# Sixty counting instructions on VectorE and on ScalarE ahead of the first batch of a matmul kernel

## Chip, cores and metric

One core of one Trainium2 chip. The metric is the device time of one execution in microseconds (us). The span is the time from the first to the last instruction in the trace; for this kernel it is some 2 us shorter than the time (260.2 beside 262.41 us in the profiled run of before).

## The reference

```python
x: (16, 768, 512) float32;  y: (16, 768, 1024) float32
np.einsum('bkm,bkn->bmn', x, y).astype(np.float32)      # (16, 512, 1024)
```

Sixteen independent matmuls. Per batch 1.57 MB of x and 3.15 MB of y are read and 2.10 MB written.

## The kernel before

SyncE issues all transfers. VectorE casts x and y to bf16, GpSimd passes the casts' signals on to PE, PE multiplies in two groups of 24 matmuls a batch (48 in all), ScalarE copies each group from PSUM to a buffer that SyncE stores. There are two input buffers, two bf16 buffers, two PSUM halves and five output buffers.

```python
# SyncE
for b in range(B):
    i = b % 2
    if b >= 2:
        nc.sync.wait_ge(cast, nx[b - 2])                 # x buffer has been cast
    wide_dma("x", xs[i][:], x_v[b], 4, True).then_inc(sx[i], 16)
    if b >= 2:
        nc.sync.wait_ge(cast, nx[b - 2] + parts(b - 2))  # y buffer has been cast
    wide_dma("y", ys[i][:], y_v[b], 2, True).then_inc(sy[i], 16)
    if b >= LAG:                                         # LAG = 4
        store(b - LAG)
# ... the last four stores follow
# VectorE
for b in range(B):
    # ... waits for the bf16 buffer (b >= 2) and for x
    nc.vector.tensor_copy(xb[:, i], xs[i][:]).then_inc(cast, 1)
    nc.vector.wait_ge(sy[i], n)
    # ... cast of y, in two parts in the last batch
# ... GpSimd, PE
# ScalarE
nc.scalar.nop().then_inc(room, 2)
for b in range(B):
    # ... waits for the output buffer (b >= NO)
    for g in range(2):
        nc.scalar.wait_ge(groups, 2 * b + g + 1)
        cp = nc.scalar.copy(ob[b % NO][...], ps[g][:])   # cut
        # ... signals
```

## Time and profile before

| | before |
|---|---|
| time, median of the first 3 runs | 262.47 us (262.26 to 262.50) |
| span of the profiled run | 260.2 us |
| bytes moved, mean rate | 109.05 MB, 419 GB/s |
| busy: PE, VectorE, ScalarE | 73%, 32%, 23% |
| first matmul, last copy starts, last store issued | 18.51, 249.35, 251.24 us |

### The profile page before, as it was taken

How to read it: one execution, taken by the hardware profiler on the slowest of the kernel's cores; microseconds unless marked ns; L12 is line 12 of the kernel's file. 1: busy time of each engine (PE TensorE's matmuls, PEld its weight loads, DVE VectorE, ACT ScalarE, POOL GpSimd, SP SyncE). 2: the span in 40 equal slices, each digit the busy share in tenths (PEclk: the TensorE clock that was granted, in tenths of full speed). 3: DMA queues.
4: the chain of work that ended last, by engine and by line, in shares of the span. 5: the costliest groups of instructions: out<-in, count | busy, mean ns of one | idle time of the engine just before them, and what ended most of it. 6: DMA issues, size and time to landing. Idle time of an engine off the chain costs nothing. (4 is left out here: it accounts for less than half of the span.)

```text
span 260.2 us, 2386 instructions
## 1 busy us (share of the span) xinstructions
PE 189.0 (73%) x768; PEld 90.4 (35%) x768; DVE 82.0 (32%) x33; ACT 61.0 (23%) x33; POOL 0.2 (0%) x4
## 2 busy tenths in 40 slices
PE   0019999997938949689494995939869196796930
PEld 0004555553513514334241352514434043352510
DVE  0271644525241152411425214252232523125000
ACT  1000432343220220403222022220412214022220
POOL 0000000000000000000000000000000000000000
PEclk9999999999995977979889597997999889797995
DMA  7998989999999999998999989999998999999995
GB/s 272 434 487 378 484 378 468 393 358 479 423 395 471 385 474 431 426 433 385 489 416 426 448 368 461 418 463 408 393 496 378 466 446 411 433 393 436 423 408 232
DMA packets 4512, 109.05 MB, mean 419 GB/s; under 512 B 768, under 2 KB 768, under 8 KB 768
## 3 DMA queue, kind: packets, MB, share of 16 engines
q1 hardware_dynamic: 4512, 109.05, 98.3%
HBM read 75.50 MB, written 33.55 MB: 419 GB/s over the span
## 5 line engine op out<-in xcount | busy, mean ns | idle before, releaser
L146 PE MATMUL ps<-yb,xb 128*128 x768 | 189.0, 412 | 60.3 <-PEq L141 58.3
L146 PEld LDWEIGHTS ps<-yb,xb 128*128 x768 | 90.4, 118 | 158.5 <-issue 93.2
L160 ACT COPY ob<-ps 128x2048 f32<-128x2048 f32 x32 | 59.8, 1868 | 189.2 <-PE ps L146 189.2
L124 DVE CAST yb<-ys 128x6144 bf16<-128x6144 f32 (+1 forms) x17 | 53.8, 3171 | 86.8 <-DMA ys<-in_y_dram 86.8
L120 DVE CAST xb<-xs 128x3072 bf16<-128x3072 f32 x16 | 28.1, 1759 | 69.4 <-DMA xs<-in_x_dram 65.2
L160 ACT ACT_TABLE_LOAD x1 | 1.3, 1283 | 1.0 <-SPq L45 1.0
L184 POOL MEMSET const-bfloat16-1.0<- 128x1 bf16 x1 | 0.1, 101 | 0.0
L184 POOL MEMSET const-uint8-127<- 128x1 uint8 x1 | 0.1, 101 | 0.0
L184 POOL MEMSET const-float32-0.0<- 128x1 f32 x1 | 0.1, 98 | 0.2 <-issue 0.2
L184 POOL MEMSET const-float32-1.0<- 128x1 f32 x1 | 0.1, 98 | 0.0
## 6 DMA issues: line engine op xcount, KB each, us to landing
ys<-in_y_dram SPq DMA_DIRECT2D x16, 3072.0 KB, 28.2
out_dram<-ob SPq DMA_DIRECT2D x16, 2048.0 KB, 32.6
xs<-in_x_dram SPq DMA_DIRECT2D x16, 1536.0 KB, 29.8
```

The lines of the kernel that those rows point to most:

```text
L120: nc.vector.tensor_copy(xb[:, i], xs[i][:]).then_inc(cast, 1)
L124: nc.vector.tensor_copy(yb[:, i, ks], ys[i][:, ks]).then_inc(cast, 1)
L146: mm = nc.tensor.matmul(ps[g][:, m, nt], x_w[:, bass.ds(s, 1), kt, mo], yb[:, bass.ds(s, 1), kt, nt * NF:(nt + 1) * NF], start=(kt == 0), ...
L160: cp = nc.scalar.copy(ob[b % NO][:, g * HB:(g + 1) * HB].rearrange("p m (t f) -> p m t f", f=NF), ps[g][:])
L184: nc = _bacc.Bacc("TRN2", target_bir_lowering=False, num_devices=1)
```

## The change

VectorE and ScalarE have nothing to do until the first loads land. The change lets each run through 60 instructions that only add 1 to a semaphore for which nobody waits. The intent is to occupy both engines' sequencers in idle time; by design no wait, transfer or arithmetic is altered. Only ScalarE's table load, which stands behind the count, comes later (5.34 instead of 0.97 us).

```diff
+    idle = ec(nc.semaphore("idle"))
...
+    for _ in range(60):
+        nc.vector.sem_inc(idle, 1)
     for b in range(B):          # VectorE's loop
...
     nc.scalar.nop().then_inc(room, 2)
+    for _ in range(60):
+        nc.scalar.sem_inc(idle, 1)
     for b in range(B):          # ScalarE's loop
```

## The prediction

> **What bounds the kernel now.** I read the page from the top: busy shares first, then the DMA queue, then the start and the end of the run in order of time, because the change touches only the start.

> ```profile
> PE 189.0 (73%) x768; PEld 90.4 (35%) x768; DVE 82.0 (32%) x33; ACT 61.0 (23%) x33; POOL 0.2 (0%) x4
> ...
> DVE  0271644525241152411425214252232523125000
> ACT  1000432343220220403222022220412214022220
> ...
> DMA  7998989999999999998999989999998999999995
> ...
> q1 hardware_dynamic: 4512, 109.05, 98.3%
> HBM read 75.50 MB, written 33.55 MB: 419 GB/s over the span
> ```

> The two engines that get the new instructions are the idle ones: VectorE (DVE) is busy 32% of the span, ScalarE (ACT) 23%, and in the first slice of 6.5 us neither has any arithmetic (ACT's 1 is its table load). The DMA row is at 8 or 9 tenths everywhere but in the first and the last slice, and the queue takes 98.3% of sixteen engines' time. The bytes bound this kernel: 109.05 MB at the measured 419 GB/s is the 260.2 us span. VectorE and ScalarE matter only where they would make the queue run dry, at its head, or make the last store late, at its tail.

> The timeline of the first 32 us, cut to the loads and the two engines (columns: start us, duration us, engine, line, what it does, and in brackets its idle time and what ended it):

> ```profile
> 0.95 0.39 SPq L71 DMA_DIRECT2D xs<-in_x_dram  x1
> 0.97 1.28 ACT L160 ACT_TABLE_LOAD   x1 [0.97 <-SPq L45]
> ...
> 2.43 0.70 SPq L71 DMA_DIRECT2D ys<-in_y_dram  x1
> 7.26 1.76 DVE L120 CAST xb<-xs 128x3072 bf16<-128x3072 f32 x1 [7.26 <-DMA xs<-in_x_dram]
> 9.05 0.47 SPq L71 DMA_DIRECT2D xs<-in_x_dram  x1
> 14.57 3.36 DVE L124 CAST yb<-ys 128x6144 bf16<-128x6144 f32 x1 [5.55 <-DMA ys<-in_y_dram]
> ...
> 25.79 1.87 ACT L160 COPY ob<-ps 128x2048 f32<-128x2048 f32 x1 [23.54 <-PE ps L146]
> ```

> All four first loads are issued by SyncE with no wait, by 2.43 + 0.70 = 3.13 us. VectorE's first cast waits for data until 7.26 us, its second until 14.57 us. ScalarE loads its table and then has nothing until 25.79 us. Those are the two windows into which the change puts its instructions. The end is set by the last batch: the chain of work that ended last names only PE and ScalarE's copies, from 222.58 us on, and neither engine's stretch there is touched.

> [...]every transfer is in q1, issued by SyncE alone, so no VectorE or ScalarE instruction issues a transfer, before or after. [...]In this trace's DMA records the instruction fetches (six packets of 8192 bytes) all end more than 7 us before the first instruction; none lies in the span.[...]

> **The change, part by part.** Nothing is removed and no wait is added: nobody waits on the new semaphore. Built, the program has exactly 60 more semaphore instructions on VectorE (17 to 77) and on ScalarE (15 to 75); the order of casts, copies, matmuls and DMAs is unchanged on every engine.

> What one costs. The only semaphore records of the two engines inside the loop are their plain waits:

> ```profile
> L119 DVEq EVENT_SEMAPHORE  x14: 21/21/21, 29.3 to 227.5; - x14
> L159 ACTq EVENT_SEMAPHORE  x11: 17/17/17, 86.9 to 244.2; - x11
> ```

> They last 21 and 17 ns. From the start of such a wait to the start of the cast or copy behind it is 63 to 65 ns on VectorE and 56 to 61 ns on ScalarE where the data was there; two semaphore instructions in a row on GpSimd stand 78 ns apart. A VectorE record is 21/17 = 1.24 times as long, so the slow estimate for VectorE is 78 x 1.24 = 97 ns.
> - VectorE: 60 x 64 = 3.8 us to 60 x 97 = 5.8 us. Its last start-up branch is at 0.77 us and ends by 0.82, so the count ends at 4.7 to 6.6 us. The first cast can start at 7.26: hidden, with 0.6 to 2.6 us to spare.
> - ScalarE: 60 x 57 = 3.4 us to 60 x 78 = 4.7 us, from 0.9 us on. The table load (1.28 us) stands behind the count in the built order, so it ends at 5.6 to 6.9 us, against a first copy at 25.79. The increment by which ScalarE frees both PSUM halves stands ahead of the count, and PE does not start before 18.51 us anyway. Hidden by some 19 us.
> - On the path: 0. The sum is 0 us.

> Even if VectorE's count overran, the first cast has slack. It may start 5.55 us late and still be done when the second cast's data comes at 14.57 us. What it releases is the third x load, issued at 9.05 us behind three loads that are still queued: the cast of the second y starts at 25.57 us on data that only then lands. So per instruction the change would cost nothing until about (7.26 + 5.55 - 0.82) / 60 = 200 ns each, twice my slow estimate.

> **The rivals.**
> - *The count overruns the first load, and the end moves with it.* For it: the first cast is the earliest thing that VectorE does, and my slow estimate leaves only 0.6 us. Against: the slack of 5.55 us just shown. It would take over 200 ns each; at 250 ns, 60 x 250 = 15 us, the first y cast would start at about 15.8 + 1.8 = 17.6 us, 3 us late, and the time would be 265 us at the most, since the queue stays fed.
> - *Instruction fetch.* VectorE's program grows from 59 to 119 instructions, ScalarE's from 57 to 117; with what the runtime puts ahead that may need one more 8192-byte packet, or two. For it: [...]if it fell in the middle of the run, one cast or copy could be late by the time of a few queued packets (1.8 us for one of 49152 bytes). Against: [...]the queue holds two further loads (28.2 us from issue to landing). 0 to 2 us, most likely 0.
> - *It helps.* [...]For it I find nothing: the first cast starts when its load is complete, and no idle time before it is put down to issue.[...]
> - [...]

> **Range and chances.** The three runs before lie within 0.24 us, so what is left is noise and the small fetch risk, upward only. I predict 262.5 us, 261.9 to 263.2. A gain of 2% would be 5.2 us, [...]by an edit that feeds no transfer sooner: chance 0.01. A loss of 2% needs a stall of over 5 us that reaches the tail: 0.02. Same: 0.97.

> **What would show it right or wrong.** Right: 60 semaphore records on each engine, VectorE's ending before 7.26 us; the first cast still within 0.1 us of 7.26 and still waiting for the load; the table load at about 4.3 to 5.6 us; DMA share 98 to 99%, first matmul at about 18.5 us, last copy at about 249.3 us. Wrong: a first cast put down to issue, an instruction fetch inside the span with a gap on VectorE or ScalarE beside it, or a tail moved by over a microsecond.

The forecast's sum on the path was 0 us, and it stands. Passages of the prediction that no trace of this case shows are cut, and the cuts marked; none of them was a term of that sum.

## More of the kernel before

The lines for the start are in the prediction. For the end, which the prediction read too quickly, here are two stretches of the kernel before. The columns are the stretch, its length, the busy time of PE, its weight loads, VectorE, ScalarE and GpSimd (with counts), the granted clock of PE as a share of full speed, the DMA share and GB/s:

```profile
236.00:242.00 6.00, 4.93 (x15) 2.12 (x16) 2.17 (x2) 0.99 (x1) 0.00 (x0) 0.72 1.02 434
...
248.00:254.00 6.00, 1.31 (x7) 0.45 (x4) 0.00 (x0) 1.86 (x1) 0.00 (x0) 1.00 0.96 410
```

The second line is the one to keep: while PE does its last seven matmuls and ScalarE its last copy, the DMA engines are 96% busy, up to 252 us with stores of earlier batches. The first says that in this run PE was granted 0.72 of its clock early in the last batch.

## The result and the profile after

262.13 us median of 6 runs (261.94 to 262.59), beside 262.32 us of before (6 runs, 262.12 to 262.50). The ratio is 0.9995, 95% interval 0.9982 to 1.0007: the same. (Ratios here are the mean time of one kernel's fast runs over that of the other's of the same rounds, so not quite the ratio of the medians quoted.)

The page of the changed kernel, its DMA row and its queues:

```profile
DMA  7999989999999999999999999999999999999995
...
q1 hardware_dynamic: 4512, 109.05, 98.3%
q14 instruction: 2, 0.02, 0.0%
```

The share of the data queue is 98.3% as before. The last line is new: two packets that fetch instructions, inside the span. The trace has them at 9.01 and 10.84 us, 8192 bytes each.

The counting instructions, as groups by line (L116 is VectorE's loop, L159 ScalarE's; durations in ns, minimum, median and maximum, then first and last start in us):

```profile
L116 DVEq EVENT_SEMAPHORE  x60: 21/21/21, 1.0 to 6.4; - x60
L159 ACTq EVENT_SEMAPHORE  x60: 17/17/17, 1.0 to 5.3; - x60
```

From start to start they stand 92.8 ns apart on VectorE and 67.5 on ScalarE, though a record is only 21 and 17 ns long. In one place ScalarE paused: 376 ns between its 59th and 60th count.

The timeline of the start (start, duration, engine, what, idle time before and what ended it):

```profile
5.34 1.28 ACT L165 ACT_TABLE_LOAD   x1 [5.34 <-issue]
7.23 1.76 DVE L123 CAST xb<-xs 128x3072 bf16<-128x3072 f32 x1 [7.23 <-DMA xs<-in_x_dram]
9.01 0.47 SPq L72 DMA_DIRECT2D xs<-in_x_dram  x1
14.91 3.36 DVE L127 CAST yb<-ys 128x6144 bf16<-128x6144 f32 x1 [5.92 <-DMA ys<-in_y_dram]
...
18.85 13.36 PE L149 MATMUL ps<-yb,xb 128*128 x52 [18.85 <-PEq L144]
```

The first cast still waits for its load and starts at 7.23 us (7.26 before). The second starts at 14.91 instead of 14.57, and the first matmul at 18.85 instead of 18.51: the second load landed a third of a microsecond later. In the casts that shift is gone from the fifth batch's second cast on; the last copy starts at 249.33 us (249.35 before).

So three things were to be tested: how much counting the start really hides and by what; whether the fetches cost anything, and where; and what the same instructions cost on the chain that ends last.

### The profile page after: what moved, and what is told of

The parts are those of the page before. It is cut to its first block, busy times and chain, and to the rows that moved or that the text cites. A ratio compares the mean times of both kernels' runs of the same rounds, so it can differ in the third digit from the quotient of the medians.

```text
span 260.2 us, 2506 instructions
## 1 busy us (share of the span) xinstructions
PE 188.3 (72%) x768; PEld 90.3 (35%) x768; DVE 82.0 (32%) x33; ACT 61.1 (23%) x33; POOL 0.2 (0%) x4
## 3 DMA queue, kind: packets, MB, share of 16 engines
q1 hardware_dynamic: 4512, 109.05, 98.3%
HBM read 75.50 MB, written 33.55 MB: 419 GB/s over the span
## 5 line engine op out<-in xcount | busy, mean ns | idle before, releaser
L123 DVE CAST xb<-xs 128x3072 bf16<-128x3072 f32 x16 | 28.2, 1760 | 69.7 <-DMA xs<-in_x_dram 65.2
## 6 DMA issues: line engine op xcount, KB each, us to landing
ys<-in_y_dram SPq DMA_DIRECT2D x16, 3072.0 KB, 28.2
```

## The experiments

Twelve kernels ran. All gave the reference's result.

| run | edit | median us | before, same rounds | ratio (95% interval) |
|---|---|---|---|---|
| c0 | semaphore only, no counts | 262.40 | 262.49 | 1.0002 (0.9989 to 1.0015) |
| v60 | 60 on VectorE | 262.34 | 262.30 | 1.0010 (0.9981 to 1.0039) |
| a60 | 60 on ScalarE | 262.51 | 262.30 | 1.0017 (0.9984 to 1.0049) |
| mid30 | 30 on each | 261.90 | 262.30 | 0.9994 (0.9972 to 1.0017) |
| tail14 | 14 and 15 | 261.79 | 262.29 | 0.9977 (0.9963 to 0.9990) |
| tail14b | the same again | 262.30 | 262.49 | 0.9991 (0.9978 to 1.0004) |
| c120 | 120 on each | 262.44 | 262.29 | 1.0000 (0.9987 to 1.0014) |
| c240 | 240 on each | 265.55 | 262.29 | 1.0121 (1.0105 to 1.0137) |
| c480v | 480 on VectorE | 288.54 | 262.29 | 1.0990 (1.0971 to 1.1009) |
| path20 | 20 on ScalarE before its last copy | 262.85 | 262.49 | 1.0018 (0.9996 to 1.0040) |
| path60 | 60 there | 263.91 | 262.30 | 1.0073 (1.0043 to 1.0102) |
| path120 | 120 there | 268.02 | 262.49 | 1.0221 (1.0194 to 1.0248) |

### How much the start hides: 120, 240 and 480 counts

```diff
-    for _ in range(60):
+    for _ in range(120):      # c120 and c240: both engines; c480v: 480 on VectorE, none on ScalarE
         nc.vector.sem_inc(idle, 1)
```

> 120 counting instructions on each of VectorE and ScalarE ahead of the loop. The trace of the changed kernel shows 92.7 ns from one to the next on VectorE and 67.5 on ScalarE, so VectorE is free at about 0.97 + 120 x 0.0927 = 12.1 us and the first cast starts near 12.2 us instead of 7.23, that is 5 us late, not waiting for its load; ScalarE is done at 9.1 us. Theory (slack): the second load of y lands only near 14.6 us, so the first matmul stays at 18.5 to 18.9 us and the time is that of the kernel before, within 0.5 us. Rival (what is not hidden is paid): 5 us longer, 267.3 us. One fetch of instructions by each of the two engines falls into the span, as with 60.

> 240 on each engine. VectorE is free at about 0.97 + 240 x 0.0927 = 23.2 us, so the first cast is 16 us late and the first matmul comes near 28.8 us instead of 18.5. Theory (the queue must stay fed): the four first loads keep the DMA engines busy until 25.6 us and the next x load is issued at about 25.1, so the queue loses 1 us or so and PE, which has 27% idle time later, catches up its 10 us: 263.3 to 265.5 us. Rival (a late first matmul moves the end): 272 us. Second rival (a late first cast moves the end): 278 us. Two fetches by each engine[...].

> 480 on VectorE alone. VectorE is free at about 45.5 us; the next x load is issued at 47.3, so the queue stands empty from 25.6 to about 48 us. Theory (the queue must stay fed): the time grows by those 22 to 24 us, 284 to 287 us, although the first cast is 38 us late. Rival (a late first cast moves the end): 300 us. Rival (PE makes up for it): under 275 us.

With 120, the timeline of c120:

```profile
12.51 1.76 DVE L123 CAST xb<-xs 128x3072 bf16<-128x3072 f32 x1 [12.51 <-issue]
...
15.03 3.36 DVE L127 CAST yb<-ys 128x6144 bf16<-128x6144 f32 x1 [0.76 <-DMA ys<-in_y_dram]
```

The first cast is 5.2 us late and no longer waits for its load: "issue" means that nothing in the profile held it, and here that is the counting. The second cast still waits for its load, 0.76 us. The time did not move, ratio 1.0000. The rival "what is not hidden is paid", 5 us longer, falls. So what hides counting is not the wait for the first load alone, but at least the time until the second one. ScalarE's own counts play no part in this: even with 240 they end at 17.7 us, and its first copy waits for PE until 36.45 us.

With 240, the first cast came at 24.02 us, 16.8 us late, and the first matmul at 29.63, 11.1 us late. The time grew by 0.0121 x 262.29 = 3.2 us only. Stretches of c240, and below it the same ones of the kernel before:

```profile
18.00:24.00 6.00, 0.00 (x0) 0.00 (x0) 0.00 (x0) 1.07 (x1) 0.00 (x0) 1.00 1.00 427
24.00:30.00 6.00, 0.37 (x1) 0.23 (x2) 5.97 (x3) 0.00 (x0) 0.00 (x0) 1.00 0.59 213
```

```profile
18.00:24.00 6.00, 5.49 (x17) 2.35 (x18) 1.76 (x1) 0.00 (x0) 0.00 (x0) 1.00 0.91 393
24.00:30.00 6.00, 6.00 (x30) 3.15 (x28) 3.36 (x1) 1.87 (x1) 0.00 (x0) 1.00 0.96 410
```

Up to 24 us the DMA engines do not notice that VectorE is absent. Then the four first loads are done, the next ones have only just been issued (25.81 and 29.08 us), and the rate falls to 213 GB/s. Against the 410 of before that is (410 - 213) x 6 us = 1.2 MB, or 2.8 us at 419 GB/s: most of the 3.2. (Summed from 0 to 36 us, c240 moved 1.5 MB less than before, or 3.6 us.) The queue's share of the whole span gives the same size, here for c240:

```profile
q1 hardware_dynamic: 4512, 109.05, 97.3%
```

The DMA engines were without data packets for 2.7% of 263.9 us, or 7.1 us, beside 1.7% of 260.2 us, or 4.4 us, before: 2.7 us more. Eleven microseconds of lateness on PE were otherwise made up. The time lies at the upper edge of my range (265.55 against 265.5).

With 480 on VectorE, the DMA row of c480v (slices of 7.17 us):

```profile
DMA  7993002899989999999999999999989899999995
GB/s 281 447 439 152 1 0 77 364 432 432 432 322 485 402 453 432 416 439 368 466 402 453 414 455 414 469 425 407 455 380 482 382 460 416 432 439 409 434 407 247
```

The queue starves in slices 4 to 8. Against a steady 432 GB/s they lack (280 + 431 + 432 + 355 + 68) GB/s x 7.17 us = 11.2 MB, or 26 us at that rate. The measured cost is 0.099 x 262.29 = 26.0 us. I had expected 22 to 24; the count itself took 45.9 us instead of 44.5 because of four pauses (next section), and the slow slice around the restart was not in my sum. The first cast was 39.7 us late and the first matmul 34.1. So the cost follows the hole in the queue, neither the lateness of the cast nor that of PE.

### Fetches: where they come from and what they cost

The two engines apart:

```diff
-    for _ in range(60):
-        nc.scalar.sem_inc(idle, 1)      # v60; a60 drops VectorE's loop instead
```

> 60 on VectorE alone. Theory: one fetch of 8192 bytes in the span instead of two, the one near 10.8 us[...]; the second y load lands up to 0.35 us late; time as before within 0.4 us. Rival: the fetches are not tied to the counts (two, or none, or at other times).

> 60 on ScalarE alone. Theory: one fetch, the one near 9.0 us, the pause of 0.31 us between ScalarE's 59th and 60th counting instruction stays, time as before within 0.4 us. Rival: as for the VectorE run. If the first y load lands late in only one of the two runs, the engine that fetches is what decides it.

Each has one fetch: v60 at 10.79 us, a60 at 9.07, where the changed kernel has 10.84 and 9.01. ScalarE's pause stays in a60 (377 ns). Neither time differs from before clear of noise. In both runs the second load is late: from the first cast's start to the second's it is 7.65 us in v60 and 7.62 in a60, 7.68 in the changed kernel with two fetches, but 7.29 to 7.38 in the eight traces of before, c0, mid30, tail14, tail14b, path20, path60 and path120, where no fetch falls into the start. So in these traces a fetch delayed that load by 0.3 us, whichever engine made it, and in the one trace of the changed kernel two do not add up. In the packets of the changed kernel, those of 24576 bytes take 912 ns (the median of 128), but the two that start where a fetch ends take 1166 and 1451 ns, and the fetch itself 309. That it is these two packets which make the load late is my reading; no run tests it.

Where the fetch is triggered, with other counts:

> 30 on each. Theory: instruction 64 or 65 is now a cast or copy in the middle of the run, so both fetches come there, between 90 and 180 us, with a pause of 0.3 us that waits hide; time as before within 0.3 us. Rival (the bound queue pays for each fetch): 0.3 to 0.6 us longer.

> 14 on VectorE and 15 on ScalarE. By the changed kernel's trace the fetch and a pause of 0.31 us came when ScalarE passed its 64th or 65th instruction, counted from the start of the program; with these counts that place is the last y cast on VectorE and the last copy on ScalarE, so the same pause and fetch fall into the last 25 us. Theory (a fetch costs about 0.3 us, in the head it is absorbed, at the tail it is not): 0.3 to 0.7 us longer than before, the last copy 0.3 us late, and one or two fetches of 8192 bytes at 236 to 256 us. Rival (fetches never matter, or come at no fixed count): as before within 0.2 us and no fetch at the tail.

```diff
-    for _ in range(60):       # both loops
+    for _ in range(30):       # mid30; tail14: 14 on VectorE, 15 on ScalarE
```

The fetches moved as the theory has it: to 152.8 and 171.1 us in mid30, to 231.7 and 248.1 us in tail14 (one of them earlier than I had said). No cost appeared: mid30 0.9994; in tail14 the last copy starts at 249.29 us (249.35 before) where I expected 0.3 us later. My expectation for tail14, that a fetch at the end must cost 0.3 us or more, fails. The run does not show that a fetch on the chain would be free: the last copy was still waiting for PE (3.25 us), and the next section finds a slack of over 1.4 us at the end, which would hide 0.3 us in any case. Instead tail14 came out 0.23% faster, with an interval clear of 1. That asked for a control and a repeat:

> The semaphore is declared, but nothing counts: the instructions of the kernel before. A control for the differences of 0.1 to 0.2% that the counting runs showed. Theory (those are noise between builds and rounds): a ratio anywhere in 0.998 to 1.002, and no fetch in the span. Rival: exactly 1.000 with a narrow interval, so that the 0.23% of the run with 14 and 15 counts is real.

> The run with 14 and 15 counts once more, as it came out 0.23% faster with an interval clear of 1, which no theory of mine explains. Noise theory: the ratio is nearer to 1 this time, 0.999 to 1.002, and fetches again near 232 and 248 us. Rival (a real gain of 0.5 us): 0.996 to 0.999 again.

The repeat gave 0.9991, with an interval that includes 1, and fetches at 231.7 and 248.5 us. The control gave 1.0002. I take the 0.23% for chance among twelve comparisons; two runs do not prove it, and a gain of 0.1 to 0.2% stays possible.

The place of the pauses is the same in every run that shows one. In c480v VectorE pauses after its 60th, 188th, 316th and 444th count, for 444 to 485 ns instead of 92.7, that is every 128 counts. ScalarE pauses after its 59th count and in c240 again after its 187th, 128 later. The trace has three records of VectorE and four of ScalarE ahead of their first counts, so by its records the first pause comes after the 63rd on both engines. It does so too in path20, path60 and path120 below, where 48 records of ScalarE stand ahead and the pause follows the 15th count. (The expectations speak of the 64th or 65th instruction.) In the kernel before, the trace has 55 records of VectorE and 54 of ScalarE in all: neither gets there. In the changed kernel VectorE's 63rd record is its last count, so whatever pause it made fell into the wait for the first load. Each pause seen has one fetch after it. In c480v the packet came 4.0 and 4.5 us after the end of the first two pauses (6.93 to 10.88 and 19.17 to 23.66 us), with data packets in the queue, and 0.7 us after the third's and fourth's (31.40 to 32.09, 43.62 to 44.29), with the queue empty. With data packets in the queue it was 3.5 to 4.5 us in all of the changed kernel, c120, c240 and c480v. The pause itself cost 372 - 67.5 = about 0.30 us on ScalarE and 0.35 to 0.40 us on VectorE. In c120 ScalarE's counts stand 72.5 ns apart instead of 67.5, for which I have no cause.

### The same counts on the chain that ends last

```diff
             nc.scalar.wait_ge(groups, 2 * b + g + 1)
+            if b == B - 1 and g == 1:
+                for _ in range(60):          # path20: 20, path120: 120
+                    nc.scalar.sem_inc(idle, 1)
             cp = nc.scalar.copy(...)          # the loops at the start are dropped
```

> The same 60 on ScalarE, but after its wait for the last matmul group and ahead of the last copy, and none elsewhere. Theory (same instructions, but on the path that sets the end): 60 x 67.5 ns = 4.05 us plus the pause of 0.31 us: 4.2 to 4.5 us longer, about 266.7 us. Rival (counting runs ahead of the wait, or costs only its 17 ns of execution): 0 to 1.1 us longer.

> 20 on ScalarE after its last wait, ahead of the last copy: 20 x 67.5 ns + 0.31 us pause = 1.65 us on the chain of PE and ScalarE. Theory (the last store waits 1.45 us or more for a DMA engine that still has older stores to write, so the chain has that much slack, and 3.0 us where PE got its full clock in the last batch): 0 to 0.4 us longer. Rival (the chain sets the end, and the run with 60 was short only by PE's clock): 1.4 to 1.8 us longer.

> 120 in the same place: 8.1 + 0.31 = 8.4 us on the chain. Theory (slack once used up, each further count is paid in full): the run with 60 plus 60 x 67.5 ns = 4.05 us, about 5.4 to 6.4 us longer than before, 267.7 to 268.7. Rival (the cost is in proportion to the count): twice that of the run with 60, 3.3 to 3.8 us longer, about 266 us.

The last batch of the kernel before, without the weight loads:

```profile
237.07 12.23 PE L146 MATMUL ps<-yb,xb 128*128 x48 [1.99 <-ACT ob L160]
...
249.35 1.86 ACT L160 COPY ob<-ps 128x2048 f32<-128x2048 f32 x1 [3.26 <-PE ps L146]
```

path60, timeline of its last batch, then two stretches:

```profile
237.00 10.73 PE L147 MATMUL ps<-yb,xb 128*128 x48 [2.20 <-PEq L142]
242.64 1.87 ACT L164 COPY ob<-ps 128x2048 f32<-128x2048 f32 x1 [5.94 <-PE ps L147]
252.15 1.87 ACT L164 COPY ob<-ps 128x2048 f32<-128x2048 f32 x1 [7.64 <-issue]
```

```profile
236.00:242.00 6.00, 5.00 (x23) 2.65 (x24) 2.10 (x2) 0.70 (x1) 0.00 (x0) 1.00 1.02 434
...
248.00:254.00 6.00, 0.00 (x0) 0.00 (x0) 0.00 (x0) 1.85 (x1) 0.00 (x0) 0.93 0.61 261
```

The count did cost what I had worked out: ScalarE's wait ended at 247.77 us and the copy started at 252.15, 4.38 us later, the pause of 372 ns included. So the rival, that counting runs ahead of the wait or costs only its execution, falls. Yet the time grew by 0.0073 x 262.30 = 1.9 us (interval 1.1 to 2.7), not 4.2 to 4.5. Two terms were missing. First, in this run PE had its full clock in the last batch (1.00 where before has 0.72), and its 48 matmuls took 10.73 instead of 12.23 us, so the last store was issued only 2.80 us later than before (254.04 against 251.24). Second, SyncE's wait for that store ended at 260.33 instead of 258.98: 1.35 us later. The remaining 1.45 us were absorbed by the DMA engines. In the kernel before they are still 96% busy at 248 to 254 us; here they fall to 61%, as they wait for the last store. The packets say it in detail: before, the engines end the last store between about 257.0 and 258.59 us, ten of them by 257.12, one at 257.4 and five only from 258.05 on. In path60 they end it within 0.2 us of each other, at 259.8 to 259.96. The packets do not name their engine; by joining packets of which one starts where another ends, I take it that the late ones were still writing older stores when the last store's first packets came at 252.1.

The absorbed part is the same in all three runs. Against the kernel before, the last store is issued 2.10, 2.80 and 6.51 us later in path20, path60 and path120, and the wait for it ends 0.64, 1.35 and 5.05 us later: 1.46, 1.45 and 1.46 us less. mid30 shows the reverse: full clock in the last batch, last store 1.62 us earlier, end only 0.10 us earlier. This is no accident of one profile. From issue to landing the last store takes 7.71 to 7.94 us in the eight traces whose last 48 matmuls took 12.1 to 12.2 us (before, after, c0, v60, tail14, tail14b, c120, c480v), 9.21 to 9.25 us in the three where they took 10.7 (a60, mid30, c240), and 6.26 to 6.28 us in the three path runs. By the times, path20 costs 0.5 us (interval -0.1 to 1.0; expected 0 to 0.4, its rival 1.4 to 1.8), and path120 5.8 us (expected 5.4 to 6.4, its rival 3.3 to 3.8). From path60 to path120 it is 5.8 - 1.9 = 3.9 us for 60 x 67.5 ns = 4.05 us: past the slack, each count is paid.

The runs of path120 spread from 266.76 to 269.32 us and those of path20 from 262.14 to 264.24, those of before in the same rounds only from 262.20 to 262.75. PE's clock in the last batch may be the reason, since with the slack used up its 1.5 us reach the end. The timed runs have no records of that batch, so this is argued and not shown; their mean granted clocks, 0.887 to 0.907 in path120, do not order with their times.

## Why the prediction was right, and where it was not

## What to carry to other kernels

Here instructions in an engine's idle time were free up to the moment at which something that the bound resource needs was issued late, well after that engine's first wait had ended: a first cast 5.2 us late cost nothing (c120), one 16.8 us late cost 3.2 us (c240). Measure it by doubling the filler until the time moves. The chain that ended last was a chain of waits and not yet the bound: with the DMA queue still full when its last transfer was issued (96% busy at 248 to 254 us), shortening or lengthening the chain by a little changed little (up to some 1.5 us were absorbed). When a few more instructions are added to an engine, look for instruction fetches in the queue list (here two packets of 8192 bytes for 60 counts on each of two engines), and judge them by the end of the run and not by their presence.
